# A modulation vector moved from VectorE to TensorE, and decays and copies moved to ScalarE, in the first mixer of a hybrid diffusion step

## The chip, the cores and the metric

One core of a Trainium2 chip runs the whole program. The metric is the device time of one execution in microseconds (us). Engines are named as the profile names them: PE is TensorE (PEld its weight loads), DVE is VectorE, ACT is ScalarE, POOL is GpSimd, SP the engine whose queue issues the loads. Each engine runs its own instructions in the order in which they were put into the program.

## The reference

Two layers, each a mixer and a convolutional feed-forward, over 512 latent and 128 context tokens of width 1024. What matters here is the first mixer and the vectors that scale it:

```python
mod = (jax.nn.silu(cvec) @ w + bias).reshape(-1, 1, 6 * D_MODEL)   # six vectors a layer, for c and for c_ctx
hs = rms_norm(xs, norm_mix_g[i]) * (1.0 + sc1s) + sh1s
os_ = ab_mixer(hs, ...)          # neighbourhood attention heads (A) and gated linear attention heads (B)
xs = xs + g1s * os_              # g1: vector 2, the mixing gate
xs = xs + g2s * conv_ffn(rms_norm(xs, g) * (1.0 + sc2s) + sh2s, ...)   # vectors 3 and 4, and 5
# B, per chunk: bcum = cumsum(log decay)
att = einsum(q_i, k_j, exp(bcum_i - bcum_j)), j <= i
k_dec = k * exp(bcum_last - bcum)          # decay to the end of the tile
s_new = exp(bcum_last) * s + k_dec^T v
o = att v + (q * exp(bcum)) s
```

## The kernel before

All activations are kept feature-major, 128 partitions by 640 tokens (512 latent, 128 context). A product in fp32 is made of three passes over a high and a low part of each operand: ACT writes the high part of a weight (`wh`, line 111), DVE the low part (`wl`, line 112), and in the first mixer every second low part is GpSimd's (`WPOOL`). Weights come 512 KB at a time through two buffers (`ws`, line 127, `NWS = 2`); a buffer is free when both parts of it are written.

The stages follow each other: `begin` (norm of the input, modulation vectors 0 and 1 on PE), `mix0` (the first mixer, `layer0`), `ffn0`, `mix1`, `ffn1`. The change is in `mix0` alone. There PE has two kinds of work. One is products with weights, kept as generators in a queue (`Fill`) and given out in small steps between the other work: `tokens_major` makes values token by token (`tm`, lines 592 to 594, copied out at 599 on DVE for odd tiles and at 601 on ACT for even ones; once for `vg`, the values of B, once for `va`, those of A), and `products` makes the gate `rg` and queries and keys (`mm`, line 153). The other is linear attention for two pairs of heads, m = 0 and 1, in the order `ORDER`: scores, states, output. `gla_scores` goes through eight levels of block size. A level takes four subtractions on DVE (`ea`, `eb`, lines 840 to 843), two exponentials on ACT (830), a product on POOL (846) and one on DVE (847), then small matmuls on PE (`lev`, 860), whose result DVE masks and POOL adds up (865, 867). The last two levels write `off` and `offx` (882, 886); ACT copies them to `att` (891, 892), and DVE copies the blocks of the diagonal from `acc` into it (895). `gla_states` makes the decays to the end of the tile, `kd` (DVE 910, ACT, POOL 912), transposes them (`kdt`), copies (`kt`) and forms the state updates (`ds`, 927). `gla_out` forms the output (`go`, 952 to 955), and ACT copies it out of PSUM (`got`, 958 and 959).

Beside all that, `modulations` makes vectors 2, 3 and 4 of layer 0 on DVE: for each of 16 pieces of 256 KB of a vector's weights (`wa`, three buffers) two multiplications with accumulated sum (line 316, written `junk` and `wa`), one for `c`, one for `c_ctx`. The vectors are first read after the attention, when the output projection is added to the residual.

The order on each engine is made when the program is built, by a scheduler that places instructions by priority and by a model of their times; on the chip it is fixed.

Of the kernel before, what the change touches and what calls it, by code (L numbers as in the profile page):

```python
# [30 lines left out]
def kernel(ctx: ExitStack, tc: tile.TileContext, a: dict, o: dict):  # L31
# [266 lines left out]
    def modulations(todo, room):  # L298
# [8 lines left out]
        for l, g in todo:  # L307
# [11 lines left out]
            for v in range(2):  # L319
                nc.vector.tensor_tensor(m[:, v, :], acc[:, :, v, 0], acc[:, :, v, 1], ALU.add)  # L320
                nc.vector.tensor_tensor(m[:, v, :], m[:, v, :], adab[:, l, g, :], ALU.add)

    def norm_scale(l, g, gi):
        s = cp.tile([P, 2, KD], F32, tag=f"A{l}{g}", name=f"A{l}{g}")
# [253 lines left out]
    def tokens_major(src, n, H, vs, tag, bufs=None, out=None):  # L578
# [5 lines left out]
        for c in range(n // 256):  # L584
            ws = [weights(src[c, q], 1024, 256) for q in range(2)]
            for t in range(5):
# [10 lines left out]
                dst = vs[t][:, 256 * c:256 * c + 256]  # L597
                if t % 2:
                    nc.vector.tensor_copy(dst, ps)
                else:  # L600
                    nc.scalar.copy(dst, ps)  # L601
# [29 lines left out]
    def layer0(H, raws):  # L631
# [36 lines left out]
        lr = C("lr")  # L668
        nc.vector.tensor_copy(halves(lr)[0:64], ps[0:64, :, 0:HN])
        side = modulations(VECTORS[0:3], lambda: T("sb", "napx", n=512, bufs=4))  # L670
        run(products([a["w_ab"][3]], H, kq_done, (("p1", "p1"),), first=3))
# [38 lines left out]
        g_vg = tokens_major(a["w_vg"], 512, H, vg, "v2")  # L710
        fill.add(g_vg)
        fill.add(products([a["w_ab"][12 + m] for m in range(4)], H, rg_done, (("mm", "po"),)))
        g_va = tokens_major(a["w_va"], 512, H, va, "v2", out=values)
# [118 lines left out]
    def gla_scores(m, k, q, F, G, fill):  # L832
# [56 lines left out]
        for e in range(2):  # L889
# [3 lines left out]
            for j in range(4):  # L893
                pj = slice(32 * j, 32 * j + 32)
                nc.vector.tensor_copy(
                    x[pj, 0:NT].rearrange("p (t i) -> p t i", i=128)[:, :, 32 * j:32 * j + 32],
                    acc[pj, 160 * e:160 * e + 160].rearrange("p (t i) -> p t i", i=32),
                )
# [3 lines left out]
    def gla_states(m, k, F, G, vg, S, fill):  # L902
# [3 lines left out]
        for d, c in ((0, F), (1, G)):  # L906
            x = C("kd")
            cvw = c[:, 0:NT].rearrange("p (t i) -> p t i", i=128)
            end = cvw[:, :, 127:128] if d == 0 else cvw[:, :, 0:1]
            nc.vector.tensor_tensor(x[:, 0:NT].rearrange("p (t i) -> p t i", i=128), end.to_broadcast([P, 5, 128]), cvw, ALU.subtract)  # L910
            expo(x[:, 0:NT], x[:, 0:NT])
            nc.gpsimd.tensor_tensor(x[:, 0:NT], x[:, 0:NT], k[:, 0:NT], ALU.mult)
# [583 lines left out]
def arrange(i):  # L1496
# [24 lines left out]
    d["ada_w01"] = aw[0, :, :, 0:2].transpose(3, 1, 0, 2, 4).reshape(KD, P, 2 * D)  # L1521
    d["ada_wt"] = np.stack([aw[l, :, :, g].transpose(2, 3, 0, 1).reshape(KD, P, D) for l, g in VECTORS])
    d["crow"] = np.concatenate([ar["c"][0], ar["c_ctx"]])[None]
    q = np.arange(P)
# [87 lines left out]
```

## Time and profile before

| | us |
|---|---|
| median of 3 runs | 1730.79 |
| lowest, highest | 1728.23, 1732.38 |
| the profiled execution | 1732.08 |
| its span in the trace | 1730.3 |
| PE busy in the span | 1640.0 (95%) |
| DVE busy in the span | 1280.7 (74%) |
| ACT busy in the span | 720.9 (42%) |

Busy shares are means over five stages with different limits; the stage of the change lies between about 45 and 375 us of the span. Matmuls overlap, so that a busy PE isn't PE at its peak. The granted clock is a share of 2.4 GHz; at 0.5 it is 1.2 GHz.

### The profile page before, as it was taken

The page shows a single profiled execution, that of the slowest core. Times are in us where ns is not written, and L with a number is a line of the kernel's source. Part 1 is how long each engine was busy: PE and PEld are TensorE (multiplying, and loading weights), DVE is VectorE, ACT ScalarE, POOL GpSimd, SP SyncE. Part 2 cuts the span into 40 slices and gives each one's busy share as a digit, 9 for nine tenths or more (in the row PEclk, how much of TensorE's full clock was granted, in tenths as well). Part 3 has the DMA queues.
Part 4 walks back from the last instruction along what each step waited for, and adds up shares of the span by engine and source line. Part 5 has one row for each costly group of instructions (what it writes and reads, how often), then busy time and mean ns, then how long its engine had stood idle before and what let it go on. Part 6 is the DMA issues. An engine that isn't in the chain of part 4 may idle for free.

```text
span 1730.3 us, 33463 instructions
## 1 busy us (share of the span) xinstructions
PE 1640.0 (95%) x13142; PEld 1565.2 (90%) x13142; DVE 1280.7 (74%) x2877; ACT 720.9 (42%) x1599; POOL 206.5 (12%) x475
## 2 busy tenths in 40 slices
PE   7978798989999999999999999899999999999997
PEld 6867787878999999999998888789999999999997
DVE  5899955775899989996656987996776644663664
ACT  4443255453533313322335566665453322331342
POOL 2134441210200000000003310100100000000001
PEclk8988889999999999999998999999999999999998
DMA  8624323322255455444232200120222222222222
GB/s 317 204 86 133 108 90 97 101 88 92 81 165 164 152 165 183 151 149 128 70 122 87 68 20 13 42 63 20 80 66 82 74 74 73 74 69 91 72 66 71
DMA packets 68014, 175.22 MB, mean 101 GB/s; under 512 B 7920, under 2 KB 9744, under 8 KB 66832
## 3 DMA queue, kind: packets, MB, share of 16 engines
q1 hardware_dynamic: 67024, 171.48, 30.7%
q8 instruction: 103, 1.69, 0.4%
q0 software_dynamic: 832, 1.60, 0.3%
q14 instruction: 55, 0.45, 0.1%
HBM read 165.71 MB, written 7.34 MB: 100 GB/s over the span
## 4 chain that ended last, share of the span: by engine, by line
PE 78%; DVE 15%; DMA 3%; ACT 2%; issue 2%; SPq 0%; POOL 0%; ACTq 0%; DVEq 0%; POOLq 0%
PE mm L153 66%; DVE junk L316 2%; PE gpo L1297 2%; DVE wa L316 2%; PE gpt L1285 1%; DVE wl L112 1%; PE gs L1276 1%; DMA wa<-in_ada_wt_dram 1%; DVE mx L1023 1%; PE gs L1277 1%; PE napo L1089 1%; PE ss L410 1%; DVE eb L847 1%; DMA x<-in_xT_dram 0%; DVE q L613 0%
## 5 line engine op out<-in xcount | busy, mean ns | idle before, releaser
L153 PE MATMUL mm<-hh,wl 128*128 128x320 f32 x2080 | 652.6, 316 | 5.3 <-DVE x L488 1.9
L153 PE MATMUL mm<-hl,wh 128*128 128x320 f32 x2080 | 648.3, 312 | 0.6 <-DVE hl L456 0.6
L153 PE MATMUL mm<-hh,wh 128*128 128x320 f32 x2080 | 641.9, 312 | 0.0
L111 ACT CAST wh<-ws 128x512 fp32r<-128x512 f32 x376 | 228.8, 615 | 447.8 <-PE mm L153 420.5
L153 PEld LDWEIGHTS mm<-hh,wl 128*128 128x128 f32 x2080 | 394.5, 190 | 15.8 <-issue 5.5
L153 PEld LDWEIGHTS mm<-hl,wh 128*128 128x128 f32 x2080 | 395.2, 190 | 3.0 <-issue 1.2
L153 PEld LDWEIGHTS mm<-hh,wh 128*128 128x128 f32 x2080 | 393.4, 190 | 0.4
L112 DVE TENSOR_TENSOR wl<-ws,wh 128x512 fp32r<-128x512 f32 x348 | 242.2, 699 | 157.4 <-ACT wh L111 156.7
L153 PE MATMUL mm<-glo,wh 128*128 128x320 f32 x704 | 217.6, 310 | 0.0
L153 PE MATMUL mm<-ghi,wh 128*128 128x320 f32 x704 | 217.3, 310 | 0.0
L153 PE MATMUL mm<-ghi,wl 128*128 128x320 f32 x704 | 216.3, 310 | 0.0
L488 DVE SCALAR_TENSOR_TENSOR x<-mm,mod,x 128x192 f32<-128x192 f32 (+2 forms) x240 | 96.6, 435 | 84.1 <-PE mm L153 83.2
L153 PEld LDWEIGHTS mm<-ghi,wl 128*128 128x128 f32 x704 | 132.0, 188 | 0.9 <-issue 0.9
L153 PEld LDWEIGHTS mm<-glo,wh 128*128 128x128 f32 x704 | 132.6, 188 | 0.0
L153 PEld LDWEIGHTS mm<-ghi,wh 128*128 128x128 f32 x704 | 132.4, 188 | 0.1
L316 DVE SCALAR_TENSOR_TENSOR junk<-wa,sb 128x512 f32<-128x512 f32 x160 | 120.4, 757 | 9.4 <-DMA wa<-in_ada_wt_dram 7.0
L316 DVE SCALAR_TENSOR_TENSOR wa<-wa,sb 128x512 f32<-128x512 f32 x160 | 113.2, 714 | 0.2
L522 POOL MEMSET u<- 128x1 f32 x88 | 8.9, 102 | 767.2 <-DVE gate L515 432.5
L525 ACT COPY u<-mm 128x320 f32<-128x320 f32 x88 | 37.8, 431 | 87.6 <-PE mm L153 83.2
L1029 ACT ACTIVATE gp<-gs,mx,rq 128x640 f32<-128x640 f32 x64 | 56.9, 889 | 36.6 <-DVE mx L1025 27.9
L592 PE MATMUL tm<-wl,hh 128*128 128x256 f32 x200 | 61.3, 312 | 8.3 <-ACT v L601 4.0
L528 ACT COPY u<-mm 128x192 f32<-128x192 f32 x88 | 28.4, 322 | 78.8 <-PE mm L153 78.8
(302 smaller groups left out, 2452.7 us busy)
## 6 DMA issues: line engine op xcount, KB each, us to landing
ws<-in_wu_dram SPq DMA_DIRECT2D x88, 512.0 KB
wa<-in_ada_wt_dram SPq DMA_DIRECT2D x160, 256.0 KB
ws<-in_wd_dram SPq DMA_DIRECT2D x32, 448.0 KB
aw<-in_ada_w_dram SPq DMA_DIRECT2D x8, 1024.0 KB
ws<-in_w_ab_dram SPq DMA_DIRECT2D x16, 512.0 KB
ws<-in_wd_dram SPq DMA_DIRECT2D x16, 512.0 KB
x<-in_xT_dram SPq DMA_DIRECT2D x16, 320.0 KB
ws<-in_w_gqa_dram SPq DMA_DIRECT2D x10, 512.0 KB
```

Source lines behind the costliest of these rows:

```text
L111: nc.scalar.copy(hi, src)
L112: eng.tensor_tensor(lo, src, hi, ALU.subtract)
L153: nc.tensor.matmul(ps, x, y[:, s], start=st, stop=sp_)
L316: nc.vector.scalar_tensor_tensor(w if v else junk, w, 1.0, cs[v, j], ALU.mult, ALU.mult, accum_out=acc[:, k, v, j:j + 1])
L410: nc.tensor.matmul(ps[0:rows, c:c + 2], part[:, t], onesd, start=True, stop=True)
L488: nc.vector.scalar_tensor_tensor(x[:, b:e], ps[:, b - HN * h:e - HN * h], gate[:, v, m:m + 1], old[:, b:e], ALU.mult, ALU.add)
L525: nc.scalar.copy(u[:, 1:321], ps)
L528: nc.scalar.copy(u[:, 321:513], ps[:, 0:192])
L592: nc.tensor.matmul(ps, hh[:, s], wlo, start=(k == 0), stop=False)
L847: nc.vector.tensor_tensor(eb[:, 0:NT], eb[:, 0:NT], q[:, 0:NT], ALU.mult)
L1029: nc.scalar.activation(dst, src, AF.Exp, bias=mx[:, i:i + 1], accum_out=sm[:, i:i + 1], **kw)
L1297: last = nc.tensor.matmul(po[64 * f:64 * f + 64, 0:128], vs[t][:, 64 * kv:64 * kv + 64], mates[f]["x"][:, 128 * t:128 * t + 128], start=(t ...
```

## The change

Vector 2 of layer 0, the mixing gate, is no longer made by `modulations` on DVE, but by a new generator, `row_modulation`, on PE: for each pair of 128 outputs two loads of 512 KB through the `ws` buffers, eight matmuls each with the 32-column conditioning tile in four column groups, a copy on ACT, two matmuls with `sel` that turn the rows back into columns, and an addition of the bias on DVE. It stands in the `Fill` queue behind the values of B. The weights are the same bytes in another layout (`ada_wr`). Besides, copies go from DVE to ACT: the odd tiles of the values in this stage, the result `lr` of the low-rank projection, and the diagonal blocks of `att`. The decays to the tile ends lose their subtraction on DVE: ACT makes exp(-c/16 + end/16) in five instructions of 128 columns, with the end as a bias that it has scaled before.

```diff
+    def row_modulation(l, g):
+
+        m = new_mod(l, g)
+        for k in range(0, KD, 2):
+            ws = [load(a["ada_wr"][k + i]) for i in range(2)]
+            ps = P1("ada")
+            for i, w in enumerate(ws):
+                for r in range(KD):
+                    j = 32 * (r % 4)
+                    nc.tensor.matmul(ps[j:j + 32, 128 * i:128 * i + 128], siluc[:, r, :], w[:, 128 * r:128 * r + 128], start=(r < 4), stop=(r >= 4))
+            row = sp.tile([P, 256], F32, tag="adarow", name="adarow")
+            nc.scalar.copy(row, ps[:, 0:256])
+            yield
+            pt = ps[:, 256:260]
+            for i in range(2):
+                nc.tensor.matmul(pt[:, 2 * i:2 * i + 2], row[:, 128 * i:128 * i + 128], sel, start=True, stop=True)
+            bias = adab[:, l:l + 1, g, k:k + 2].to_broadcast([P, 2, 2])
+            nc.vector.tensor_tensor(m[:, :, k:k + 2], pt.rearrange("p (i v) -> p v i", i=2), bias, ALU.add)
+            yield
...
-                if t % 2:
+                if t % 2 and stage_[0] != "mix0":
                     nc.vector.tensor_copy(dst, ps)
...
-        nc.vector.tensor_copy(halves(lr)[0:64], ps[0:64, :, 0:HN])
-        side = modulations(VECTORS[0:3], lambda: T("sb", "napx", n=512, bufs=4))
+        nc.scalar.copy(halves(lr)[0:64], ps[0:64, :, 0:HN])
+        side = modulations(VECTORS[1:3], lambda: T("sb", "napx", n=512, bufs=4))
...
         fill.add(g_vg)
+        fill.add(row_modulation(0, 2))
...
-                nc.vector.tensor_copy(
+                nc.scalar.copy(
                     x[pj, 0:NT].rearrange("p (t i) -> p t i", i=128)[:, :, 32 * j:32 * j + 32],
...
-            nc.vector.tensor_tensor(x[:, 0:NT].rearrange("p (t i) -> p t i", i=128), end.to_broadcast([P, 5, 128]), cvw, ALU.subtract)
-            expo(x[:, 0:NT], x[:, 0:NT])
+            e16 = sp.tile([P, 5], F32, tag="e16", name="e16", bufs=4)
+            nc.scalar.mul(e16, end.rearrange("p t i -> p (t i)"), 1.0 / 16.0)
+            for t in range(5):
+                s = slice(128 * t, 128 * t + 128)
+                nc.scalar.activation(x[:, s], c[:, s], AF.Exp, bias=e16[:, t:t + 1], scale=-1.0 / 16.0)
```

The scheduler makes a new order of it. Line numbers of the changed kernel are 20 to 24 higher. On DVE, in the scores of the second pair of heads (m = 1), this stood before, with the modulation's `junk` and `wa` between the steps of a level:

```order
L865 TENSOR_TENSOR acc<-lev,mask_112 128x160 x2
L847 TENSOR_TENSOR eb<-eb,kqg 128x640
L599 COPY v<-tm 128x256
L316 SCALAR_TENSOR_TENSOR junk,adacc<-wa,sb 128x512
L112 TENSOR_TENSOR wl<-ws,wh 128x512
L316 SCALAR_TENSOR_TENSOR wa,adacc<-wa,sb 128x512
L847 TENSOR_TENSOR eb<-eb,kqg 128x640
L112 TENSOR_TENSOR wl<-ws,wh 128x512
L316 SCALAR_TENSOR_TENSOR junk,adacc<-wa,sb 128x512
L316 SCALAR_TENSOR_TENSOR wa,adacc<-wa,sb 128x512
L865 TENSOR_TENSOR acc<-lev,mask_112 128x160 x2
```

and this stands there now (L886 is the former L865, L868 the former L847, L861 to L864 are the four subtractions):

```order
L886 TENSOR_TENSOR acc<-lev,mask_112 128x160 x2
L868 TENSOR_TENSOR eb<-eb,kqg 128x640 x2
L886 TENSOR_TENSOR acc<-lev,mask_112 128x160 x2
L861 TENSOR_TENSOR ea<-cum 128x20x16
L862 TENSOR_TENSOR ea<-cum 128x20x16
L863 TENSOR_TENSOR eb<-cum 128x20x16
L864 TENSOR_TENSOR eb<-cum 128x20x16
L868 TENSOR_TENSOR eb<-eb,kqg 128x640
L886 TENSOR_TENSOR acc<-lev,mask_112 128x160 x2
```

No multiplication of a modulation is left in the second pair's scores. In the first pair's (m = 0) they stay as dense as before, since vectors 3 and 4 move forward into the places that vector 2 had; and the additions of `row_modulation` (L340) come in between, here the last two of the four:

```order
L868 TENSOR_TENSOR eb<-eb,kqg 128x640
L340 TENSOR_TENSOR mod_1195<-ada,adab 128x2x2
L316 SCALAR_TENSOR_TENSOR junk,adacc<-wa,sb 128x512
...
L316 SCALAR_TENSOR_TENSOR wa,adacc<-wa,sb 128x512
L112 TENSOR_TENSOR wl<-ws,wh 128x512
L886 TENSOR_TENSOR acc<-lev,mask_112 128x160 x2
L340 TENSOR_TENSOR mod_1195<-ada,adab 128x2x2
L868 TENSOR_TENSOR eb<-eb,kqg 128x640
```

The `wl` here is the first low part of the gate's weights (`rg`). On PE the same place, from the second level of the first pair on, now reads as follows (L332 are the matmuls of `row_modulation` with the weights, L338 those with `sel`, L881 the levels):

```order
L881 MATMUL lev<-eb,ea 32x32 x32
L338 MATMUL ada<-sel,adarow 128x2 x2
L881 MATMUL lev<-eb,ea 32x32 x33
L332 MATMUL ada<-ws,siluc 32x128 x8
L881 MATMUL lev<-eb,ea 32x32 x15
L332 MATMUL ada<-ws,siluc 32x128 x8
L881 MATMUL lev<-eb,ea 32x32 x32
L338 MATMUL ada<-sel,adarow 128x2 x2
L881 MATMUL lev<-eb,ea 32x32 x8
L332 MATMUL ada<-ws,siluc 32x128 x16
L881 MATMUL lev<-eb,ea 32x32 x12
L338 MATMUL ada<-sel,adarow 128x2 x2
```

Before, the products of `rg` (L153 `mm`) stood between these levels, 58 of them ahead of the fourth; they now come after the fifth, 120 up to the end of the first pair's `off` (143 before). In the second pair's stretch PE has 204 `tm` and 72 `mm` where it had 240 and 49; the other 36 `tm` fall behind the last `off`.

## Rows read from the trace of the kernel before

**Rows 1.** The page's busy time of engines in the whole span: engine, busy us, share, instructions.

```profile
PE 1640.0 (95%) x13142; PEld 1565.2 (90%) x13142; DVE 1280.7 (74%) x2877; ACT 720.9 (42%) x1599; POOL 206.5 (12%) x475
```

**Rows 2.** Busy time in five stretches of the first mixer: start and end, length, then PE, PEld, DVE, ACT, POOL busy (instructions), granted PE clock, share of the DMA engines, GB/s. The cuts are: DVE's first modulation work, the first level of the first pair, the end of its `off`, the first level of the second pair, the end of its `off`, the first scores of A.

```profile
54.50:111.40 56.90, 51.22 (x413) 47.36 (x412) 54.62 (x128) 24.35 (x46) 9.71 (x6) 0.94 0.54 176
111.40:163.00 51.60, 37.38 (x703) 34.62 (x701) 51.60 (x100) 16.66 (x31) 26.12 (x16) 0.85 0.28 93
163.00:176.50 13.50, 13.50 (x171) 12.52 (x170) 13.37 (x30) 6.08 (x13) 7.04 (x4) 0.93 0.48 145
176.50:233.00 56.50, 44.75 (x761) 41.29 (x761) 50.49 (x109) 15.37 (x27) 24.14 (x18) 0.82 0.29 96
233.00:266.20 33.20, 31.14 (x290) 28.45 (x286) 15.96 (x32) 22.08 (x43) 14.27 (x13) 1.00 0.30 101
```

**Rows 3.** What PE waited for from 62 to 262 us: who, for whom, us in total, times, longest.

```profile
PE lev L860 <- DVE eb L847: 14.2, 6, 5.2
PE tm L592 <- ACT v L601: 4.0, 3, 2.0
PE offx L882 <- DVE acc L865: 2.9, 1, 2.9
PE ds L927 <- ACT kt L922: 2.7, 1, 2.7
```

**Rows 4.** DVE's work from 163 to 233 us, grouped by line and shape: count, busy us, mean ns of one, idle before.

```profile
L316 DVE SCALAR_TENSOR_TENSOR junk<-wa,sb 128x512 f32<-128x512 f32 x14 | 13.8, 996 | 0.0
L316 DVE SCALAR_TENSOR_TENSOR wa<-wa,sb 128x512 f32<-128x512 f32 x15 | 13.7, 921 | 0.0
L847 DVE TENSOR_TENSOR eb<-eb,kqg 128x640 f32<-128x640 f32 x7 | 6.3, 897 | 0.0
L910 DVE TENSOR_TENSOR kd<-cum 128x640 f32<-128x640 f32 x2 | 2.7, 1368 | 0.0
L895 DVE COPY att<-acc 32x160 f32<-32x160 f32 x8 | 2.5, 310 | 0.1
L599 DVE COPY v<-tm 128x256 f32<-128x256 f32 x4 | 1.7, 414 | 4.2 <-PE tm L594 4.2
```

**Rows 5.** PE in order of time: start, length, line, what. First `mm` and `tm` in a row at the full clock, a set of `ds`, a level, then a level after a wait, with `tm` behind it.

```profile
165.09 0.31 PE L153 MATMUL mm<-hl,wh 128*128 128x320 f32 x1
165.24 0.31 PE L153 MATMUL mm<-hh,wh 128*128 128x320 f32 x1
...
174.25 1.09 PE L927 MATMUL ds<-v,kt 128*64 128x128 f32 x16
176.00 0.28 PE L594 MATMUL tm<-wh,hh 128*128 128x256 f32 x1
176.12 0.28 PE L592 MATMUL tm<-wl,hh 128*128 128x256 f32 x1
...
186.96 0.89 PE L860 MATMUL lev<-eb,ea 64*32 64x32 f32 x80
...
203.22 1.08 PE L860 MATMUL lev<-eb,ea 64*32 64x32 f32 x80 [4.92 <-DVE eb L847]
205.03 0.41 PE L592 MATMUL tm<-wl,hh 128*128 128x256 f32 x1
205.25 0.41 PE L593 MATMUL tm<-wh,hl 128*128 128x256 f32 x1
```

**Rows 6.** PE in order of time in the stage `begin`, where modulation vectors are made in the form that the change uses (there 256 columns wide, with eight `ada` matmuls of the program in 16 rows of the trace).

```profile
45.04 1.07 PE L286 MATMUL ada<-aw,siluc 128*32 128x256 f32 x16
46.04 0.41 PE L153 MATMUL mm<-hl,wh 128*128 128x320 f32 x1
46.30 0.31 PE L153 MATMUL mm<-hh,wh 128*128 128x320 f32 x1
46.44 0.31 PE L153 MATMUL mm<-hh,wl 128*128 128x320 f32 x1
...
47.03 0.50 PE L291 MATMUL ada<-sel,adarow 128*128 128x2 f32 x4
```

**Rows 7.** First DVE in order of time, the products of the fourth and fifth level of the first pair. Then the queue of loads: a load of `ws` on the chain of work (start, us), and what SP waited for from 60 to 262 us before it could issue `wa` (L313) and `ws` (L127).

```profile
143.04 2.22 DVE L847 TENSOR_TENSOR eb<-eb,kqg 128x640 f32<-128x640 f32 x2
...
176.99 3.52 DMA ws<-in_w_ab_dram
...
SPq L313 <- DVE wa L316: 84.7, 38, 10.4
SPq L127 <- DVE wl L112: 37.1, 11, 8.1
```

**Rows 8.** ACT's work from 40 to 266 us by line and shape: copies of a tile of values, small copies, an activation with a bias operand of 128 columns, the exponential of `kd` in one piece.

```profile
L601 ACT COPY v<-tm 128x256 f32<-128x256 f32 x12 | 4.3, 362 | 15.4 <-PE tm L594 15.4
...
L830 ACT ACTIVATE kd<-kd 128x640 f32<-128x640 f32 x4 | 3.0, 740 | 3.1 <-DVE kd L910 3.1
...
L447 ACT ACTIVATE hh<-h,fm 128x128 fp32r<-128x128 f32 x4 | 1.6, 388 | 0.0
...
L892 ACT COPY att<-offx 128x128 f32<-128x128 f32 x4 | 0.9, 291 | 0.0
```

**Rows 9.** The end of the linear attention on ACT in order of time: start, length, line, what, idle before and what ended it.

```profile
233.26 1.08 ACT L891 COPY att<-off 128x512 f32<-128x512 f32 x2 [1.84 <-PE off L886]
...
239.18 1.48 ACT L830 ACTIVATE kd<-kd 128x640 f32<-128x640 f32 x2 [1.71 <-DVE kd L910]
...
241.93 1.28 ACT L771 ACT_TABLE_LOAD   x1
243.22 2.62 ACT L771 ACTIVATE rg<-rg 128x640 f32<-128x640 f32 x4
...
246.78 0.57 ACT L958 COPY got<-go 128x512 f32<-128x512 f32 x1
```

More of the change, by code (lines that the diff above doesn't have):

```diff
@@ L1522, in arrange @@
     d["ada_wt"] = np.stack([aw[l, :, :, g].transpose(2, 3, 0, 1).reshape(KD, P, D) for l, g in VECTORS])
+    d["ada_wr"] = aw[0, :, :, 2].transpose(2, 1, 0, 3).reshape(KD, P, D)
     d["crow"] = np.concatenate([ar["c"][0], ar["c_ctx"]])[None]
```

## The prediction

> **What bounds the kernel now.** The page comes first: PE is busy for 95% of the span, DVE for 74% [rows 1], so that over the whole PE is the bound and work taken from DVE is worth nothing. But the change lies in one stage, so the second view is the busy time of that stage cut into stretches [rows 2]. There the order is turned round. From 54.5 to 233 us DVE is busy for 170.1 of 178.5 us, and for all of the scores of the first pair (51.60 of 51.60); PE has 37.38 of these 51.60 and 44.75 of the next 56.50, at a granted clock of 0.85 and 0.82, that is partly at 1.2 GHz. In the last stretch, 233 to 266.2, it is PE again (31.14 of 33.20, clock 1.00, DVE 15.96). The third view is the waits of PE [rows 3]: the longest total, 14.2 us, is a level's matmuls waiting for DVE's product `eb`. The chain between them goes round: PE's level, DVE's mask, DVE's subtractions, ACT's exponentials, DVE's product, PE's next level; and between these steps DVE's queue holds modulation work that nobody waits for until the output projection.
>
> A second loss hangs on the wait. After the 4.92 us without work at 198 to 203, the `tm` start 0.22 us apart, where they were 0.12 apart before [rows 5]: the clock granted has fallen to its lower level and the next work takes twice its time. So a wait costs more than its length.
>
> **Second pair of heads, 163 to 233: the gain.** Here DVE loses most. Rows 4 give 29 multiplications of `wa` and `junk` (27.5 us), of which the new order leaves none behind the first pair's products; also 8 copies of `att`'s first pair (2.5), two `kd` (2.7) and 4 copies of values (1.7). That is 34.4 of DVE's 63.9 us in these 70 us [rows 2, 4]; 29.5 are left. DVE can't be the bound then.
>
> What PE must do there, at the full clock, from starts that follow each other [rows 5]: a `tm` each 0.117 us (an average of 0.12 and 0.11), an `mm` each 0.147, a level 0.89, a set of `ds` 1.09. The order gives 204 `tm` (23.9), 72 `mm` (10.6), six levels (5.3), two sets of `ds` (2.2); eight transposes and the 60 matmuls of `off` would be 4.6 at the 0.068 of a `ds`, and I take 3.3, since `off` has the smaller tiles. Sum 45.3, where the stretch took 70.0. That is the lower end. The upper end is the loop: a level needs four subtractions, two exponentials, product, matmuls, mask. With the product of 0.90 [rows 4], the level of 0.89 [rows 5] and two exponentials of 0.74 (the rate of a 640-column one in rows 8), and subtractions and mask of together some 2.6 to 3, that is about 6.5 us a level if nothing overlaps. PE has 42 `mm` and a level ahead of the first mask, some 8 us; six such rounds follow, and 3 for `off`: some 50, with handovers 56. Since the order pairs levels (two products stand together in the new rows), PE's own queue should be longer than the loop most of the time, and I take 48.5: **21.5 us less**, with 14 and 24.7 as the ends. No copy of values on ACT changes that: ACT is busy for 21.5 of these 70 us [rows 2].
>
> **First pair, 111.4 to 163: nearly nothing, some loss.** The 47 multiplications before it and 17 of its own stay in DVE's queue, as the order shows: the space of vector 2 is filled by 3 and 4. So DVE's chain is shorter only by four copies, `lr` and low parts that come later: some 5 us up to the products that stood at 143.04 [rows 7]. PE, though, has lost its filling. The gate's weights `rg` come through the same two `ws` buffers as the eight loads of `row_modulation`, and those are issued in SP's queue behind `wa` loads, which wait for DVE (84.7 us of waiting in 38 times, rows 7). A load takes 3.52 us [rows 7]. The order lets DVE make the first low part of `rg` about 7.5 us of its own work (four multiplications, four subtractions, a product) after those products, so between 141.5 at the rates without contention and 145.5 at today's. I take 143.5. From there PE has 120 `mm` (17.6), one level and `off` (3.4), and starts at the lower clock, as after the wait in rows 5 (1 us): the end is at 165, against 163.0. **2 us more**; the ends are 2 less (all rg ready, DVE's chain ends it) and 7 more (145.5, another load late).
>
> The matmuls of the modulation themselves cost little. In `begin` a weight tile of 256 columns took 1.07 us for its eight matmuls in four column groups, and two selecting matmuls 0.50 [rows 6]; with half the columns, eight tiles and four pairs are 8 x 0.54 + 4 x 0.50 = 6.3 us of PE in a stretch in which it waits for DVE anyway. Without that cover it would be 6.3 us on the path. Behind such a group the first `mm` took 0.41 instead of 0.31 us, and the next started 0.26 later, not 0.14 [rows 6], 0.12 us a switch; with 16 switches 1.9 us, hidden in the same place. The Trainium skill ("TensorEngine Tiling (Array Packing)", Key Properties) says that a change of tiling mode drains TensorE; this speaks against mixing these groups with levels and full tiles. Rows 6 show such a drain as 0.12 us, and the page gives no time of its own, so by both the sum stays as it is as long as PE waits there.
>
> **End of the linear attention, 233 to 266: a loss.** PE is the bound, so the 36 `tm` that move here cost 36 x 0.117 = 4.2 us, the lower end. ACT's queue grows too. Before the third head's matmuls the outputs `got` must be copied out, at 246.78, 13.8 us after the last `off` [rows 9]. Into ACT's queue ahead of that copy come eight copies of `att` (0.291 to 0.388 each by rows 8, so 2.3 to 3.1, where DVE had them), two `kd` in ten pieces of 0.29 to 0.39 for the 1.48 of now (1.4 to 2.4 more) and two copies of values (0.72); what leaves is the waiting for DVE's `kd`, 1.71 [rows 8, 9]. Net 2.7 to 4.5, on a part that PE fills with 28 of the `tm`. 24 `mm` that stood ahead of the third head come after it. I take **5.5 us more**, with 4.2 and 8. On all this the skill speaks against the change: "ScalarE: Activation LUTs", Rules for kernel authors, would have additions and multiplications on VectorE and not on ScalarE. The rows differ for such sizes in fp32: a tile of values took 0.414 us on DVE and 0.362 on ACT [rows 4, 8]. By the page's "up to about 3×" (stated for bf16, so an estimate) the eight copies of `att` would take 7.4 us instead of 2.5, and the sum below would be -9; by the rows it isn't so, and I go by the rows.
>
> **Sum.** -21.5 + 2 + 5.5 = -14.0. The work behind is the same in both, and PE-bound; I leave it at 0, between -1 and +3, since its loads follow `go` as before. The profiled execution took 1732.08, 1.8 over its span; so 1718.1. It stands 1.3 above the median of the runs, 1730.79, so against that the forecast is **1717**. The bounds added up give -23.7 and +4.
>
> **Rivals.** What a measurement of this kernel can tell from no change is about 0.2%, 3.5 us.
> (a) *The loop is the bound of the second pair.* PE waits at nearly every level still; 56 us instead of 48.5 and 6.5 less in all: 1723.5. For it speaks that PE executes in order and stands between mask and product; against it the pairs of levels.
> (b) *More is won.* Both pairs at their best, PE without waits at the full clock: 1708. Against it: the first pair's multiplications stay.
> (c) *The gain is handed back*: in neighbourhood attention, which starts earlier but for its values `va` must wait, since their last tiles now end behind `off`, are written out and read back: 1729.
> (d) *Slower: the additions of the modulation hold DVE.* The four L340 stand in DVE's queue between products and masks. Each waits for PE's selecting matmuls, these for two loads through the `ws` ring, those for SP, which waits for `wa`, which DVE frees: a circle in which one late load stops the levels of the first pair and `rg` together. Each us that a load takes over 3.5 counts about three times (three rounds follow each other: weights 5 and 6, 7 and 8, then `rg`). It decides from 14 + 3.5 us on, that is from loads of over 9 us each; then 1736. Against it: the load in rows 7 took 3.52.
>
> **Chances.** Forecast (1713 to 1721) 0.53; (a) 0.18; (b) 0.12; (c) 0.08; (d) 0.09. Faster by more than 0.2%: 0.53 + 0.18 + 0.12 = 0.83; the same 0.08; slower 0.09. The range that leaves out (d), most of (c) and the far part of (b) is 1705 to 1728; the likeliest case alone is 1713 to 1721.
>
> **What the profile after would show.** Right: from the end of the first pair's `off` to that of the second some 48 us, at a clock near 1, DVE busy for about 30; PE's wait for L868 in it gone to 2 or 3 us; the end of the first `off` at 163 to 167, with PE waiting for levels up to about 143; `got` some 17 us behind the last `off`; the first scores of A at about 252 in place of 266. Wrong: DVE waiting at L340 for several us, or the first `off` after 170; PE waits of 3 us and more at every level of the second pair; ACT full behind the last `off`; or a distance from the first scores to the end that isn't 1464 us any more.

## The result, and the profile after

The change made the kernel 0.9% slower: 1747.41 us (median of 5 runs, 1743.55 to 1750.79) against 1730.83 (5 runs beside it); ratio 1.0090, 95% interval 1.0076 to 1.0103. The forecast was 1717. The profiled execution took 1744.28, and its span is 12.2 us longer than before. It is one of the two fastest of the five, so the stretches below account for 12 us; the medians differ by 16.6.

The page of after, busy time of the engines in the span [rows 1]:

```profile
span 1742.5 us, 33684 instructions
PE 1652.5 (95%) x13286; PEld 1575.2 (90%) x13286; DVE 1246.6 (72%) x2784; ACT 734.1 (42%) x1648; POOL 201.6 (12%) x475
```

DVE has 34 us less to do, PE 12.5 more. Next the three stretches of the first mixer after, cut at the ends of the two last `off` and at the first scores of A, and below them the whole way from 54.5 to these scores, before and after (columns as in [rows 2]). The first begins at 111.40 us in every kernel; in the kernel before that is DVE's first mask of the first pair, just behind its first level:

```profile
111.40:172.50 61.10, 47.33 (x813) 41.71 (x811) 48.29 (x94) 19.08 (x37) 25.19 (x17) 0.78 0.40 131
172.50:229.60 57.10, 52.24 (x917) 48.16 (x917) 39.13 (x59) 25.95 (x58) 27.48 (x20) 0.94 0.17 57
229.60:276.70 47.10, 39.21 (x317) 36.72 (x317) 11.49 (x24) 27.85 (x63) 16.04 (x15) 0.89 0.34 112
...
54.50:266.25 211.75, 178.00 (x2323) 164.27 (x2321) 186.06 (x394) 84.54 (x159) 81.34 (x57) 0.90 0.37 121
54.50:276.69 222.19, 188.25 (x2470) 171.44 (x2469) 151.31 (x301) 99.14 (x209) 76.47 (x58) 0.89 0.37 122
```

The first pair takes 61.1 us instead of 51.6 (+9.5; forecast +2), the second 57.1 instead of 70.2 (-13.1; forecast -21.5), the end of the linear attention 47.1 instead of 33.0 (+14.1; forecast +5.5), all that lies behind 1.8 more. These add up to the 12.3 of the span. The last two rows say it at once: DVE lost 35 us of work, and PE's time without work stayed, 33.75 and 33.94 us (length less busy), while its busy time grew by 10.25.

PE's waits from 62 to 277 us after [rows 3]:

```profile
PE lev L881 <- DVE eb L868: 10.4, 3, 5.5
PE mm L153 <- ACT v L621: 4.7, 1, 4.7
PE tm L612 <- DVE wl L112: 4.3, 2, 2.2
PE mm L153 <- DVE wl L112: 3.4, 1, 3.4
PE ada L332 <- DMA ws<-in_ada_wr_dram: 2.6, 2, 2.3
```

The wait for `eb` fell by 3.8 us, and those of [rows 3] for `acc` (2.9) and `kt` (2.7) are gone; the wait of `tm` for `wl` has doubled, and the three of `mm` and `ada` are new.

**The end.** PE in order of time behind the last `off`, then ACT in the same time [rows 9]:

```profile
239.81 0.66 PE L944 MATMUL kdt<-ident,kd 128*128 128x128 f32 x4
245.14 0.64 PE L153 MATMUL mm<-hh,wl 128*128 128x320 f32 x1 [4.67 <-ACT v L621]
245.57 0.47 PE L153 MATMUL mm<-hl,wh 128*128 128x320 f32 x1
245.84 0.47 PE L153 MATMUL mm<-hh,wh 128*128 128x320 f32 x1
...
251.06 0.31 PE L153 MATMUL mm<-hl,wh 128*128 128x320 f32 x1
251.21 0.31 PE L153 MATMUL mm<-hh,wh 128*128 128x320 f32 x1
```
```profile
239.64 0.74 ACT L851 ACTIVATE qd<-cum 128x640 f32<-128x640 f32 x1
240.40 1.28 ACT L792 ACT_TABLE_LOAD   x1
241.69 2.62 ACT L792 ACTIVATE rg<-rg 128x640 f32<-128x640 f32 x4
244.22 0.60 ACT L111 CAST wh<-ws 128x512 fp32r<-128x512 f32 x1
244.72 0.36 ACT L621 COPY v<-tm 128x256 f32<-128x256 f32 x1
```

36 `tm`, the last tile of A's values and half of the one before, now stand behind the last `off`. The last one's copy comes on ACT at 244.72, behind the table load and the gate's four activations; the next `mm` needs the bank that it frees and stands still for 4.67 us. This tile is an even one, so its copy was ACT's in the kernel before too; only its place is new. Then 21 `mm` start 0.27 us apart, where they are 0.15 apart at the full clock (granted clock 0.50 from 245.1 to 250.6, 1.00 from 251): 2.5 us more behind a wait of 4.7. A second, smaller pair (a wait of 1.75 for `kl`, and 13 `mm` at the lower clock) follows at 270 us.

### The profile page after: what moved, and what is told of

Its sections match the earlier page's. It is cut to its first block, busy times and chain, and to the rows that moved or that the text cites. A ratio compares the mean times of both kernels' runs of the same rounds, so it can differ in the third digit from the quotient of the medians.

```text
span 1742.5 us, 33684 instructions
## 1 busy us (share of the span) xinstructions
PE 1652.5 (95%) x13286; PEld 1575.2 (90%) x13286; DVE 1246.6 (72%) x2784; ACT 734.1 (42%) x1648; POOL 201.6 (12%) x475
## 4 chain that ended last, share of the span: by engine, by line
PE 81%; DVE 11%; ACT 3%; DMA 2%; issue 2%; SPq 0%; POOL 0%; ACTq 0%; DVEq 0%; POOLq 0%
PE mm L153 68%; PE gpo L1321 2%; PE gpt L1309 2%; PE gs L1300 1%; DMA wa<-in_ada_wt_dram 1%; DVE junk L316 1%; PE gs L1301 1%; DVE wl L112 1%; PE napo L1113 1%; PE ss L430 1%; DVE wa L316 1%; DVE mx L1047 1%; PE tm L612 1%; DMA x<-in_xT_dram 1%; PE tm L614 0%
## 5 line engine op out<-in xcount | busy, mean ns | idle before, releaser
L153 PE MATMUL mm<-hh,wl 128*128 128x320 f32 x2080 | 656.0, 317 | 13.6 <-ACT v L621 4.7
L153 PE MATMUL mm<-hl,wh 128*128 128x320 f32 x2080 | 651.1, 314 | 1.4 <-DVE hl L476 1.4
L153 PE MATMUL mm<-hh,wh 128*128 128x320 f32 x2080 | 643.7, 313 | 0.0
L153 PEld LDWEIGHTS mm<-hh,wl 128*128 128x128 f32 x2080 | 397.1, 191 | 24.7 <-issue 7.7
L153 PEld LDWEIGHTS mm<-hl,wh 128*128 128x128 f32 x2080 | 397.8, 191 | 5.1 <-issue 2.0
L153 PEld LDWEIGHTS mm<-hh,wh 128*128 128x128 f32 x2080 | 395.7, 191 | 0.3
L112 DVE TENSOR_TENSOR wl<-ws,wh 128x512 fp32r<-128x512 f32 x348 | 243.2, 701 | 188.6 <-ACT wh L111 184.3
L153 PE MATMUL mm<-ghi,wh 128*128 128x320 f32 x704 | 217.8, 310 | 0.0
L153 PE MATMUL mm<-glo,wh 128*128 128x320 f32 x704 | 217.7, 310 | 0.0
L153 PE MATMUL mm<-ghi,wl 128*128 128x320 f32 x704 | 215.7, 310 | 0.0
L153 PEld LDWEIGHTS mm<-ghi,wl 128*128 128x128 f32 x704 | 132.0, 188 | 0.9 <-issue 0.9
L153 PEld LDWEIGHTS mm<-glo,wh 128*128 128x128 f32 x704 | 132.8, 189 | 0.0
L153 PEld LDWEIGHTS mm<-ghi,wh 128*128 128x128 f32 x704 | 132.7, 189 | 0.1
L316 DVE SCALAR_TENSOR_TENSOR junk<-wa,sb 128x512 f32<-128x512 f32 x144 | 101.8, 709 | 10.9 <-DMA wa<-in_ada_wt_dram 8.0
L316 DVE SCALAR_TENSOR_TENSOR wa<-wa,sb 128x512 f32<-128x512 f32 x144 | 98.3, 687 | 0.3
L612 PE MATMUL tm<-wl,hh 128*128 128x256 f32 x200 | 57.6, 300 | 6.0 <-DVE wl L112 4.3
```

Of the source, the lines that this page charges most:

```text
L112: eng.tensor_tensor(lo, src, hi, ALU.subtract)
L153: nc.tensor.matmul(ps, x, y[:, s], start=st, stop=sp_)
L316: nc.vector.scalar_tensor_tensor(w if v else junk, w, 1.0, cs[v, j], ALU.mult, ALU.mult, accum_out=acc[:, k, v, j:j + 1])
L612: nc.tensor.matmul(ps, hh[:, s], wlo, start=(k == 0), stop=False)
```

## The experiments

The experiments were run three rounds beside the kernel before (e17 and e18 five), whose medians were 1730.3 to 1731.8. The runs of one kernel lie up to 13 us apart (e14: 1732.6 to 1746.1). The right half comes from one profile each: the three stretches cut as above, and the distance from the first scores to the end of the span. A profiled run can lie 4.7 us from its kernel's median (e14), and e10 and e18, which are the same program, differ by 3.3 us in the first pair; so differences of 3 us in one stretch prove nothing by themselves.

| kernel | median us | ratio to before, 95% | first pair | second | end | behind |
|---|---|---|---|---|---|---|
| before | 1730.8 | | 51.6 | 70.2 | 33.0 | 1464.0 |
| after | 1747.4 | 1.0090 (1.0076 to 1.0103) | 61.1 | 57.1 | 47.1 | 1465.8 |
| e1 row modulation alone | 1734.9 | 1.0028 (1.0016 to 1.0040) | 53.8 | 55.9 | 46.4 | 1465.5 |
| e2 moves to ACT alone | 1741.6 | 1.0065 (1.0048 to 1.0081) | 53.7 | 70.7 | 36.2 | 1464.4 |
| e3 after, values on DVE | 1737.8 | 1.0046 (1.0031 to 1.0061) | 58.9 | 55.5 | 47.2 | 1464.5 |
| e4 after, row behind `rg` | 1752.0 | 1.0136 (1.0107 to 1.0165) | 53.4 | 70.0 | 46.7 | 1464.9 |
| e5 no vector 2 | 1724.7 | 0.9965 (0.9951 to 0.9978) | 49.4 | 59.2 | 33.0 | 1465.4 |
| e6 row matmuls three times | 1743.2 | 1.0074 (1.0059 to 1.0089) | 64.0 | 55.3 | 45.3 | 1463.2 |
| e7 values alone | 1738.9 | 1.0048 (1.0033 to 1.0063) | 52.1 | 68.5 | 38.5 | 1468.1 |
| e8 decays, `att`, `lr` | 1736.3 | 1.0036 (1.0018 to 1.0053) | 55.0 | 70.1 | 33.2 | 1468.6 |
| e9 row, 16 steps | 1729.0 | 0.9999 (0.9985 to 1.0012) | 54.9 | 61.1 | 33.0 | 1466.7 |
| e10 row in one piece | 1722.3 | 0.9961 (0.9948 to 0.9974) | 58.2 | 57.4 | 33.0 | 1460.6 |
| e11 after, 16 steps | 1736.3 | 1.0035 (1.0017 to 1.0053) | 63.3 | 58.3 | 33.2 | 1468.7 |
| e12 e11, values on DVE | 1734.2 | 1.0020 (1.0008 to 1.0032) | 59.1 | 63.2 | 34.7 | 1464.6 |
| e13 after, row in one piece | 1732.0 | 1.0005 (0.9990 to 1.0020) | 61.3 | 56.3 | 34.7 | 1464.5 |
| e14 decays alone | 1739.9 | 1.0051 (1.0031 to 1.0071) | 53.0 | 66.3 | 36.3 | 1466.2 |
| e15 `att` alone | 1737.3 | 1.0032 (1.0017 to 1.0047) | 52.7 | 72.8 | 37.1 | 1460.5 |
| e16 `lr` alone | 1734.0 | 1.0016 (1.0003 to 1.0029) | 53.3 | 68.3 | 33.0 | 1462.4 |
| e17 before, 16 steps | 1733.7 | 1.0020 (1.0010 to 1.0031) | 52.5 | 68.5 | 33.0 | 1466.6 |
| e18 e10 once more | 1721.2 | 0.9944 (0.9930 to 0.9957) | 54.9 | 57.5 | 33.0 | 1462.7 |

**The two halves (e1, e2).** e1 is the kernel before with `row_modulation`, `VECTORS[1:3]` and `ada_wr` alone; e2 is the change without these three.

> Only the row modulation of vector 2 goes to TensorE; all copies and decays stay where the kernel before has them. Theory P (placement: in the first pair the row modulation stands where the gate's products filled TensorE, which costs some 9.5 us there; VectorE's relief gives some 13 us back in the second pair; the end of the linear attention loses little without the moves to ScalarE): 1726 to 1734 us, the first pair's last off at about 172. Rival R (the row modulation on TensorE is the whole loss, the moves to ScalarE help): 1742 to 1750.

> The copies and decays go to ScalarE, vector 2 stays on VectorE. Theory P (the wait for a copy of values on ScalarE at the end of the linear attention, 4.7 us and the lower clock behind it, comes from these moves, and pays back what VectorE saves): 1727 to 1737. Rival R (the moves help, the row modulation is the loss): 1715 to 1724.

Each half loses by itself, by 0.28% and 0.65%; together that is 0.93%, and the change lost 0.90%. e1 came out just above its range for P, far from R; e2 above even P's. In e1 the first pair ends 2.1 us later, as the prediction has it, so P's 9.5 there were not the row modulation's; nearly all its loss is at the end (46.4 instead of 33.0). In e2 nothing is won in the second pair. Why work taken from a full DVE wins nothing shows there, first ACT, then PE in order of time:

```profile
188.80 0.74 ACT L850 ACTIVATE ea<-ea 128x640 f32<-128x640 f32 x1 [10.41 <-DVE ea L861]
189.60 0.74 ACT L850 ACTIVATE eb<-eb 128x640 f32<-128x640 f32 x1
192.36 0.74 ACT L850 ACTIVATE ea<-ea 128x640 f32<-128x640 f32 x1 [2.02 <-DVE ea L861]
193.00 0.35 ACT L621 COPY v<-tm 128x256 f32<-128x256 f32 x1
```
```profile
183.99 0.28 PE L614 MATMUL tm<-wh,hh 128*128 128x256 f32 x1
193.41 0.58 PE L612 MATMUL tm<-wl,hh 128*128 128x256 f32 x1 [9.14 <-ACT v L621]
193.79 0.42 PE L613 MATMUL tm<-wh,hl 128*128 128x256 f32 x1
```

At 184.3 two tiles of A's values are complete, the first of them since 181.5, and the third needs the first one's bank. ACT does nothing from 178.4 to 188.8; but the copy stands behind exponentials that wait for DVE's subtractions. PE waits 9.14 us for an idle engine. ACT's 42% say how much it has to do, not when it comes to an instruction. The copy at 193.00 isn't one that was moved: the first tile is even, and its copy was ACT's before, at 182.45. New is how late DVE comes to the second pair's first subtraction, at 187.37 instead of 176.93. The multiplications ahead of it, before, then in e2:

```profile
L316 DVE SCALAR_TENSOR_TENSOR junk<-wa,sb 128x512 f32<-128x512 f32 x38 | 34.4, 909 | 4.3 <-DMA sb<-in_crow_dram 2.2 <-DMA wa<-in_ada_wt_dram 1.9
L316 DVE SCALAR_TENSOR_TENSOR wa<-wa,sb 128x512 f32<-128x512 f32 x38 | 27.9, 744 | 0.2
...
L316 DVE SCALAR_TENSOR_TENSOR junk<-wa,sb 128x512 f32<-128x512 f32 x46 | 39.6, 865 | 7.4 <-DMA wa<-in_ada_wt_dram 7.3
L316 DVE SCALAR_TENSOR_TENSOR wa<-wa,sb 128x512 f32<-128x512 f32 x45 | 35.9, 811 | 0.3
```

76 became 91: in the new order the room that the moved work left on DVE is filled with modulation work, ahead of what ACT, and through ACT PE, waits for. No run holds these multiplications in their old places, so what the moves alone would win is open. The Trainium skill ("PSUM — Partial Sum Buffer", Engine vs sequencer instructions) calls ScalarE's queue strictly first in, first out; these rows agree. The Trainium skill's "Perfetto Trace Analysis", Optimizing Scalar/DVE Operations, says that moving work to ScalarE may make sense when VectorE is saturated; here VectorE was [rows 2], and e2 is slower by 0.65%.

**Parts of the change undone (e3, e4).** e3: `if t % 2:` again for the copies of values. e4:

```
         fill.add(g_vg)
-        fill.add(row_modulation(0, 2))
         fill.add(products([a["w_ab"][12 + m] for m in range(4)], H, rg_done, (("mm", "po"),)))
+        fill.add(row_modulation(0, 2))
```

> The changed kernel with the odd tiles of the values copied on VectorE again. Theory V (the values' copies behind ScalarE's queue cost the 4.7 us wait at 240 to 245 us and about 2.6 us at the lower clock behind it): 1738 to 1741, with no wait of TensorE for a copy of values between the last off and the first scores of A. Rival (another copy or the decays on ScalarE take the place, the wait comes back elsewhere): 1745 to 1749.

> The changed kernel with the row modulation queued behind the gate's products instead of ahead of them. Theory P (the gate's products fill the first pair's waits again): the first pair's last off comes at 160 to 165 instead of 172.5, and the time is 1735 to 1740. Rival (what the first pair wins, the second loses, since VectorE then has its modulation work no earlier done and TensorE lacks filling there): 1745 to 1749.

e3's time, 1737.8, is 0.2 us below theory V's range, but not for its reason: the end is as long as after, with a wait of 4.41 us for a copy of an even tile, which ACT had before too. e4 gives the first pair its filling back (53.4), and the second loses all that it had won: the rival, and worse than it put it. Row modulation and `rg` can change places, the same stage pays.

**What DVE's relief is worth, and what PE's work costs (e5, e6).**

```
-        side = modulations(VECTORS[0:3], ...)      e5: VECTORS[1:3], and vector 2 is its bias
-                for r in range(KD):                e6, on e1
+                for r in list(range(KD)) * 3:
```

> The kernel before, with vector 2 not made at all (its 32 multiplications on VectorE are left out and the bias stands in for it; nothing goes to TensorE): the whole relief of VectorE without its price. Prediction on record (the relief is worth some 20 us where VectorE was the bound): 1709 to 1718. Theory W (TensorE's work of the stage is fixed, so that only its idle time can be won: with the row modulation it fell by 6.7 us and was paid for with 7.7 us of work): 1722 to 1728.

> The row modulation alone, with its eight matmuls of every weight tile made three times (loads, copies and additions as they are): some 8.6 us more of TensorE by the prediction's 0.54 us for eight. If the matmuls lie in TensorE's waits, as the prediction on record has it: 1733 to 1737, as with one. Theory W (work given to TensorE counts in full, wherever it stands in the stage): 1742 to 1746; at the lower clock, up to 1752.

Both times are theory W's. Without vector 2 at all the kernel gains 0.35%, 6.1 us: all that 32 multiplications, some 30 us of DVE by [rows 4], are worth in this order (the profiled run, the second fastest of six, is 12 us shorter). And most of what is put into TensorE's waits is not hidden: three times the matmuls cost 8.3 us over e1 by the medians and 8.0 by the ratios. That this is the 8.6 of the prediction's price is luck, for the matmuls took longer, first in e1, then in e6:

```profile
L332 PE MATMUL ada<-ws,siluc 128*32 128x128 f32 x128 | 6.6, 314 | 3.5 <-DVE mod L340 2.4 <-DMA ws<-in_ada_wr_dram 1.1
...
L332 PE MATMUL ada<-ws,siluc 128*32 128x128 f32 x384 | 18.7, 298 | 3.8 <-DMA ws<-in_ada_wr_dram 3.7
```

From 54.5 us to the first scores PE is 12.1 us more busy in e6 than in e1 (192.59 and 180.49), and its time without work falls by 3.6 (from 32.44 to 28.84). So some of the work fell into waits, and the rest moved what stands behind it: PE's waits are there because its next instruction isn't ready, and work handed out ahead of that instruction can delay it too.

**The moves one by one (e7, e8, e14 to e16).** Each is the kernel before with one edit of the change's diff (e8 with three).

> The kernel before, with the odd tiles of the values copied on ScalarE in the first mixer. Theory V (the values' copies stand behind other work in ScalarE's queue, and TensorE has no free bank until they are made): 1736 to 1741, with a wait of TensorE for such a copy of over 4 us. Rival (the loss belongs to the other moves, which lengthen ScalarE's queue): 1728 to 1733.

> The kernel before, with the decays, the copies of the diagonal of att and lr on ScalarE, and the values left as they are. Theory V: 1728 to 1734 (the changed kernel with its values on VectorE stood 2.9 us above the row modulation alone). Rival (these moves lengthen ScalarE's queue and cause the waits): 1736 to 1741.

> The kernel before with the decays to the tile ends made by ScalarE in ten pieces. By the rows of before, 1.4 to 2.4 us more of ScalarE ahead of the copy got, 2.7 us less of VectorE: 1728 to 1733. If the decays are what costs in the three moves together: 1734 to 1737.

> The kernel before with the diagonal blocks of att copied on ScalarE. By the rows of before 2.3 to 3.1 us more of ScalarE ahead of the copy got, which TensorE waited for by 0.6 us: 1730 to 1734. If these copies are what costs in the three moves together: 1734 to 1737.

> The kernel before with the one copy of lr on ScalarE, 0.8 us of VectorE at about 75 us of the span. By its length nothing measurable: 1729 to 1732. If the order that the scheduler makes new from so small a change moves the time by itself: outside of 1727 to 1734.

Every one loses, values 0.48%, decays 0.51, `att` 0.32, `lr` 0.16. e7's time is V's, but its longest wait for a copy of values is 2.3 us; the 4.1 us wait is for `got`. e8 fell into the rival's range, e14 and e15 above both of theirs, and e16, at 1734.03, on the bound from which the new order would do it. The parts do not add up: decays, `att` and `lr` are 0.99% one by one and 0.36 together, and `lr`, one copy of 0.8 us long before the levels, can't cost 2.8 us by its length. So it is likely that a part of each is the new order that the scheduler makes, and that 3 us by that alone are possible; no run changes the order alone, and how much of the decays' and `att`'s loss is order and how much ACT's queue is not settled.

**The steps of the queue (e9 to e13, e17, e18).** `Fill` hands out steps, not time. `row_modulation` yields eight times, and all behind it in the queue comes eight steps later: the last tile and a half of A's values (six steps of 6 `tm` and two ends) are eight steps. Two ways to undo that:

```
-ROFF = 12
+ROFF = 16                       e9 on e1, e11 on after, e12 on e3, e17 on before
...
     row_modulation:             e10 and e18 on e1, e13 on after
-            yield
             pt = ps[:, 256:260]
...
-            yield
+        return
+        yield
```

> The row modulation alone, and the queue gives out 16 steps instead of 12 behind each pair's levels, 8 in all, as many as the row modulation takes. In the order the last two tiles of A's values (36 tm) then stand in front of the second pair's last off again. Theory S (the tail's loss of 13 us comes from these two tiles: 4.2 us of work that only moves, a wait of 3.6 us for their copy, 1.8 us for kl, and some 4 us of mm at the lower clock): first scores of A some 33 us behind the last off instead of 46.4, and 1724 to 1729 us. Rival (TensorE waits as long elsewhere): 1732 to 1736.

> The row modulation alone, handed out in one piece that takes no step of the queue: the other way to the same place of the values' tiles (36 tm in front of the last off), but with the gate's products earlier beside the first pair's levels (141 mm instead of 120). Theory S: 1724 to 1729, first scores some 33 us behind the last off. Rival (the place of the row modulation in the first pair costs what the tail wins): 1732 to 1738.

> The whole change, with 16 steps instead of 12 behind each pair's levels. Theory S: the wait for a copy of values at the end goes, and with it the loss behind it: 1736 to 1741. Theory V (the copies on ScalarE bring a wait of their own in the second pair, as they did without the row modulation): 1743 to 1748.

> The whole change with 16 steps instead of 12 and the odd tiles of the values on VectorE again. Theory S and V together: 1727 to 1732, no wait of over 2 us behind the last off. Rival (both took away the same wait, so it counts once): 1735 to 1739.

> The whole change with the row modulation handed out in one piece, without steps of the queue. If the steps are what made the change slower: 1721 to 1727, as the row modulation alone in this form took 1722.3. If the moves to ScalarE cost by themselves, whatever the row modulation does: 1733 to 1738 (1722.3 and the 10.9 that they cost alone, or a little more).

> The kernel before with 16 steps instead of 12 behind each pair's levels, no other edit. In it no tile of the values stood behind the last off, so by theory S there is nothing to win: 1729 to 1734. If the steps help by themselves: 1722 to 1726, and what the repaid kernels won was not the tail.

> The row modulation in one piece once more, on whatever chip this falls, with five rounds: 1720 to 1726 and a ratio below 0.998 if it beats the kernel before; 1727 to 1733 if the first measurement was a lucky one.

In the six runs with the row modulation (e10 and e18 are one program) the end falls from 46 or 47 us to 33 to 35, the 13 us of theory S; e9, at 1729.0, is at the upper end of its range and level with the kernel before by the ratio; e10 is below its range. e17, the same steps without row modulation, is slower by 0.2%, so it isn't the steps as such. The whole change in one piece (e13), between its two cases, is as fast as the kernel before; between it and the change stand two `yield` lines and 0.85%, 15 us. The row modulation alone in one piece beats the kernel before twice, by 0.39 and 0.56%. Its stretches (e10), then from 54.5 to the first scores e5, e10 and e18:

```profile
111.40:169.60 58.20, 44.46 (x802) 40.29 (x802) 51.97 (x98) 19.24 (x35) 25.73 (x17) 0.82 0.40 129
169.60:227.00 57.40, 52.41 (x932) 48.20 (x932) 42.40 (x71) 21.76 (x41) 29.37 (x22) 0.97 0.20 62
227.00:260.00 33.00, 30.90 (x282) 28.31 (x281) 15.93 (x33) 22.07 (x43) 14.34 (x13) 1.00 0.33 114
...
54.50:252.95 198.45, 174.14 (x2318) 159.48 (x2317) 162.02 (x322) 83.82 (x157) 79.84 (x57) 0.93 0.32 106
54.50:259.97 205.47, 180.16 (x2469) 163.94 (x2468) 163.48 (x330) 87.39 (x164) 76.61 (x59) 0.93 0.38 125
54.50:256.75 202.25, 177.89 (x2462) 161.76 (x2461) 162.75 (x326) 86.29 (x162) 76.77 (x57) 0.93 0.37 125
```

Here PE's time without work falls, from 33.75 us in the kernel before to 25.31 (24.36 in e18), with about as much busy (2.2 more in e10, 0.1 less in e18). Against e5, PE is 6.0 more busy and the first scores are 7.0 later in e10, and 3.75 and 3.8 in e18: the vector's price on TensorE, paid in full in both. That by the ratios neither is slower than e5 (0.9961 and 0.9944 against 0.9965) is not explained: the profiled run of e5 was 4.5 us below its median, and behind the scores, which no edit touches, single profiles differ by up to 8 us. The moves to ACT still cost on top: e13 stands 0.44% above e10. e12 came out between its two cases: it is 0.15% below e11, so values on DVE and the repaid steps saved mostly the same thing. The steps are not all of why the tiles moved. Two more orders, built and not run, show it: with eight empty steps in the queue of the kernel before the 36 `tm` stay in front of the last `off`; with eight empty steps in e5, where DVE has no multiplications of vector 2, they fall behind it, and in e5 itself they don't. So in these orders it takes the steps and DVE's relief together.

## Why the prediction was wrong, point by point

The forecast was 14.0 us less, and the profile has 12.3 more. Of the difference of 26.3, 8.4 lie in the second pair, 7.5 in the first, 8.6 at the end of the linear attention and 1.8 behind it. Of the signs of being wrong that the prediction names, two came: the first `off` after 170 (172.5), and ACT full behind the last `off`, busy for 17.66 of the 17.8 us up to 247.4. The end is nearly as long in e1, though, which has no moves (46.4 against 47.1).

**What bounds the kernel now: half right.** The waits of [rows 3] and the full DVE of [rows 2] are there. But "DVE is the bound of these stretches" was read as "what DVE loses is won". From 54.5 us to the first scores PE is busy for 178 of 211.75 us; at most the other 33.75, and what the lower clock costs, were to be had, and the forecast took 21.5 of it in one stretch.

**Second pair, -21.5: the mechanism right, the size wrong (-13.1; below the bound of -14).** It took 55 to 58 us in most kernels with the row modulation ahead of `rg` (61 and 63 in e9 and e12). The step that failed is that PE's own queue would be longer than the loop most of the time since levels come in pairs, so that 3.2 us over the sum would do. The first pair of levels after, DVE, then POOL, then PE:

```profile
195.06 0.48 DVE L861 TENSOR_TENSOR ea<-cum 128x320 f32<-128x320 f32 x1
195.46 1.85 DVE L862 TENSOR_TENSOR ea<-cum 128x320 f32<-128x320 f32 x1
198.50 3.36 DVE L868 TENSOR_TENSOR eb<-eb,kqg 128x640 f32<-128x640 f32 x2
```
```profile
195.26 1.69 POOL L867 TENSOR_TENSOR ea<-ea,kqg 128x640 f32<-128x640 f32 x1 [1.29 <-ACT ea L851]
198.24 1.54 POOL L867 TENSOR_TENSOR ea<-ea,kqg 128x640 f32<-128x640 f32 x1 [1.28 <-ACT ea L851]
```
```profile
200.60 1.08 PE L881 MATMUL lev<-eb,ea 64*32 64x32 f32 x80 [4.17 <-DVE eb L868]
204.12 0.41 PE L612 MATMUL tm<-wl,hh 128*128 128x256 f32 x1
204.34 0.41 PE L613 MATMUL tm<-wh,hl 128*128 128x256 f32 x1
...
206.87 0.28 PE L613 MATMUL tm<-wh,hl 128*128 128x256 f32 x1
```

A pair puts eight subtractions ahead of its two products, so PE waits 4.17 us once for both, rival (a)'s loop at one place. To the sum of 45.3, of which the forecast made 48.5, come 4.9 us of waits, 5.2 for `tm` (29.1 instead of 23.9; the lower clock until 206.6), 0.4 for `mm` and 1.5 for the small matmuls (12.3 instead of 10.8): 57.3. The prediction priced the lower clock in the first pair and left it out here. Its prices for DVE's steps, from the kernel before, were too low as well: a product took 1.34 us on average instead of 0.90, the four subtractions of a level 3.34 instead of 2.64, and DVE was busy for 39.1 us of the stretch instead of about 30. The multiplications were gone from DVE, but the steps that were left met POOL's products, as in the rows above (last section).

**First pair, +2: the number right for the row modulation (e1: +2.1), in part by luck, and wrong for the change (+9.5).** In e1 the gate's first `mm` started 4 us earlier than forecast, and what follows it took 4 us longer. (The prediction's terms add up to 165.5, not 165; and its lower bounds to -23.5, not -23.7. Neither changes anything.) For the change, the statement that DVE's chain gets shorter by what goes to ACT failed. Multiplications ahead of the gate's first `wl`, first in e1 up to 139.4 us, then after up to 145.9:

```profile
L316 DVE SCALAR_TENSOR_TENSOR junk<-wa,sb 128x512 f32<-128x512 f32 x28 | 22.7, 814 | 2.3 <-DMA wa<-in_ada_wt_dram 2.1
L316 DVE SCALAR_TENSOR_TENSOR wa<-wa,sb 128x512 f32<-128x512 f32 x27 | 18.0, 678 | 0.2
```
```profile
L316 DVE SCALAR_TENSOR_TENSOR junk<-wa,sb 128x512 f32<-128x512 f32 x31 | 23.8, 768 | 6.2 <-DMA wa<-in_ada_wt_dram 3.5 <-DMA sb<-in_crow_dram 2.7
L316 DVE SCALAR_TENSOR_TENSOR wa<-wa,sb 128x512 f32<-128x512 f32 x30 | 20.0, 680 | 0.2
```

55 became 61, as 76 became 91 in e2: the room that the moved work left was filled with modulation work, ahead of what PE waited for. With the moves the first pair is longer in every pair of kernels here (e11 and e9, e13 and e10 or e18, e3 and e1). So the gate's first `mm` starts at 145.94 (e1: 139.47; forecast 143.5, bound 145.5):

```profile
145.94 0.64 PE L153 MATMUL mm<-hh,wl 128*128 128x320 f32 x1 [3.38 <-DVE wl L112]
...
151.44 0.47 PE L153 MATMUL mm<-hh,wl 128*128 128x320 f32 x1
...
152.55 0.31 PE L153 MATMUL mm<-hh,wl 128*128 128x320 f32 x1
```

Start 2.4 us late; the lower clock lasts to 152 and costs 2.6 us instead of 1 (22 `mm` of 0.12 more); and level and `off`, which come in pieces between the `mm`, take the rest up to 172.5, about 6 us instead of 3.4. Multiplications done earlier gave nothing back: DVE then stood idle, 15.95 us up to 179.94, as its next instruction waited for a weight:

```profile
179.94 0.69 DVE L112 TENSOR_TENSOR wl<-ws,wh 128x512 fp32r<-128x512 f32 x1 [15.95 <-ACT wh L111]
```

**Matmuls of the modulation "hidden": wrong.** The price was too low: 7.1 us for those with the weights and 3.5 for those with `sel`, 10.6 instead of 6.3; from 126 to 141 us, where half of them ran, in pieces between the levels, the granted clock was 0.50. And the cover was mostly not there (e6: 3.6 of 12.1 us). The uncovered 6.3 us stood in the prediction as a case and not in the sum.

**End of the linear attention, +5.5: wrong (+14.1, beyond the bound of 8).** The 36 `tm` took some 4.8 us by their starts (priced 4.2), and `got` came 15.9 us behind the last `off`, forecast 17. The step that failed is the path: PE didn't wait for `got` but for the copy of the last tile behind the gate's activations (4.7), then ran at the lower clock (2.5), and did both again at `kl` (1.75 and 1.6); with the `tm` that is 15.3, where the stretch grew by 14.1. This one term is what e9, e10 and e13 take away.

**Behind, 0: held within its bounds** (1.8 in the profile). Over all kernels it lies between 1460.5 and 1468.7, though no edit touches that part, so 1.8 says nothing.

**Rivals.** (d) ended on the right side with 1736 but by another circle: `ws` loads of the row modulation cost waits of 2.6 us in all, and PE didn't wait for L340 (in e1 a wait of 7.6 us ends at L340, but the product ahead of it on DVE had ended only 0.07 us before). (a) has about the second pair's time (56, measured 57.1) but not its way: PE waited at two levels of it, not at nearly every one. None was "ACT's queue waits for DVE and PE for ACT". All three errors point the same way: each stretch was costed with the other engines on time.

## What to carry to other kernels

Before counting a relief as won, add up the bounding engine's busy time from the first point that the change touches to the first that needs it all; only its time without work can be won, and work given to it was hidden in its waits only in small part. An engine that is 42% busy is no free engine when its queue is in order: look at what stands ahead of an instruction there and whom that waits for. Where a scheduler makes the order, look at what it puts into the room that a move frees. Where work is handed out in steps, new work that takes steps can push the rest back; see what falls over the next boundary.

## What was not expected of the hardware

A wait cost its length and more: behind 4.67 us without work 21 `mm` ran 0.12 us longer each (2.5 us), and behind 4.17 us `tm` started 0.21 us apart for 5 us, both at a granted clock of 0.50, which is 1.2 GHz. In these rows the extra doesn't grow with the wait: behind the 9.14 us of e2 it was about 1.4 (15 `tm` some 0.21 us apart). And a subtraction of 0.48 us on DVE took 1.85 when it began while POOL multiplied (195.46 and 195.26 above). The Trainium skill ("SBUF — State Buffer", SBUF: two separate sides) has an exclusive lock on a port pair shared by the two engines; the rows fit that: 195.46 + 1.85 is 0.36 us behind POOL's end at 196.95, though spans on POOL are rough. For loops in which both work, the product and subtractions of [rows 4, 7] are to be priced with it.
